# Cross attention's values as seven block products, and recurrence queries with the weights held stationary, in a one-layer decoder kernel

## The chip, the cores and the metric

The kernel runs on one core of a Trainium2 chip. The metric is the device time of one execution in microseconds (us), the median of three timed runs. A profiled execution gives the trace that is read here; its span is the time between the first and the last instruction of the trace.

## The reference

One layer of a hybrid decoder on 256 tokens of width 1024, in float32. What matters here are two of its many products: the queries of the recurrence (`q_b`, 1024 of the 9216 columns of `w_in`) and the values of cross attention to 256 memory tokens (the second half of `wkv`).

```python
xn = rmsnorm(h, norm_mix_g)
q_a, k_a, v_a, q_b, f_b, i_b, og_b, g_a, g_b = split_cols(xn @ w_in)
y_a = moba_attention(q_a, k_a, v_a, positions) @ w_br_attn
y_b = hgrn2(q_b, f_b, i_b, og_b, lb, norm_g) @ w_br_hgrn     # uses silu(q_b) * dk**-0.5
merged = sigmoid(g_a) * y_a + sigmoid(g_b) * y_b
h = x + merged @ w_out
# cross attention, 4 heads of 256
q = rmsnorm(h, norm_x_g) @ wq
kv = rmsnorm(mem, norm_mem_g) @ wkv; k, v = kv[..., :1024], kv[..., 1024:]
p = softmax(q k^T * 256**-0.5);  h = h + (p v) @ wo
h = h + swiglu(rmsnorm(h, norm_ffn_g));  out = rmsnorm(h, final_norm_g)
```

## The kernel before

Every product with a weight keeps float32 accuracy by splitting both factors into a high and a low part of a shorter format, and adding hi·hi, hi·lo and lo·hi on TensorE (PE). The weights lie in DRAM as chunks of 128 x 2048 floats (1 MB). A chunk is loaded by SyncE's queue (SP) into one of three `raw` buffers, ACT copies it into `hi` (two instructions of 128 x 1024, L210), and VectorE (DVE) subtracts into `lo` (two, L211). There are three pairs of `hi`/`lo`. `nxt()` hands out a chunk and lets the chunk two places further on be prepared, so the load of chunk m waits for the `lo` of chunk m-3 (same `raw`), and the `hi` of chunk m waits for PE to be done with chunk m-3 (same `hi`). The list `HEAD` is the order of the 64 chunks ahead of the feed-forward part.

Two routines use a chunk. In `gemm_t` the tokens are stationary and 512 columns of weights move: 24 matmuls of 512 columns, written `pst` (L272 to L274). In `gemm_f` the weights are stationary: 16 pairs of matmuls, one of 512 columns in which the tokens' hi and lo parts stand side by side (L287) and one of 256 (L288), written `psf`; the result has the features on the partitions, and DVE adds its two halves.

- Recurrence queries: two `gemm_t`, four chunks; ACT's Silu by token; then 16 transposes on PE (L486, the function `turned`) put features on the partitions, and DVE and ACT write `QP` and `QQ`.
- Cross attention runs in this order: four `gemm_f` for the keys (here F0 to F3; evictions `ku` on ACT, `kx` on DVE, `kxh` on ACT, `kxl` on GpSimd, which is POOL), one `gemm_t` for half of the values, four `gemm_f` for the queries (Q0 to Q3, the same evictions with `qxh`, `qxl`), and one `gemm_t` for the other half of the values. The scores `xs` of head c are computed behind Q(c+1), those of head 3 in the middle of the last `gemm_t`. DVE takes the row maximum (two instructions on L1046, each with a read of its accumulator), ACT the exponential (L1050), DVE the reciprocal and the scaling of `xp` (L1054), and PE transposes `xp` into `xT` (L1060), one chunk after `xs`. Then come the products with the values, `xo`, and the output weights.

The feed-forward part uses sums of its weight blocks, which `block_sums()` makes in DRAM during the part ahead of it: ACT's queue copies a chunk (L225, L229), and POOL's queue adds another one to it (an accumulating DMA, L231): 15 copies and 15 accumulations. One such step is issued at some of the calls of `nxt()`.

PE's order is the program's. On ACT and DVE, and on POOL for the later half, a scheduler sets the order when the program is built; on the chip each engine then runs its own list strictly in order, DMA issues included. So an instruction that waits holds up all behind it on its engine.

Of the kernel before, what the change touches and what calls it, by code (L numbers as in the profile page):

```python
# [10 lines left out]
F32 = mybir.dt.float32  # L11
F32R = mybir.dt.float32r
# [120 lines left out]
def build(tc, A, out):  # L133
    nc = tc.nc
    V, SC, G, PE, SY = nc.vector, nc.scalar, nc.gpsimd, nc.tensor, nc.sync
    with ExitStack() as ctx:
# [45 lines left out]
        def prep(tags=None, raw=None):  # L182
# [17 lines left out]
            for c in range(sent if 0 < i < len(PIECES) else 0):  # L200
                a = slice(c * 2048 // sent, (c + 1) * 2048 // sent)
                SY.dma_start(raw[:, a], piece(A["w"][i], a))
            if sent == 1:
                SY.dma_start(raw, A["w"][i])
            for c in range(pieces):
                a = slice(c * n, (c + 1) * n)
                if i == 0:
                    SY.dma_start(raw[:, a], piece(A["w"][i], a))
                    yield
                SC.activation(hi[:, a], raw[:, a], AF.Copy)  # L210
                V.tensor_tensor(lo[:, a], raw[:, a], hi[:, a].bitcast(F32), op=ALU.subtract)  # L211
# [7 lines left out]
        summed = [[dram.tile([128, 2048], F32, name="sum%d_%d" % (g, i), tag="sum%d_%d" % (g, i))  # L219
                   for i in range(3)] for g in range(len(PAIRS))]  # L220

        def block_sums():
            for g, (a, b) in enumerate(PAIRS):
                for i in range(2):
                    tc.keep_in_program_order(SC.dma_start(summed[g][i], A["w"][AT_CHUNK["I", b, 0]]))  # L225
                    yield 1
                for i, u in enumerate((("I", a, 0), ("I", b, 1), ("I", b, 1))):
                    if i == 2:
                        tc.keep_in_program_order(SC.dma_start(summed[g][2], summed[g][0]))  # L229
                        yield 1  # L230
                    tc.keep_in_program_order(G.dma_start(  # L231
                        summed[g][i], A["w"][AT_CHUNK[u]], accum_op=ALU.add, max_dma_last_dim=8192))
                    yield 1
# [47 lines left out]
        def gemm_f(X2, evict):  # L281
            w = by_k(nxt(), 8)
            for m in range(2):
                a = slice(m * 128, (m + 1) * 128)
                ps = mm.tile([128, 2, 256], F32, name="psf", tag="mm")
                for k in range(8):
                    PE.matmul(ps, w[0][:, k, a], X2[:, :, k], start=k == 0, stop=False)  # L287
                    PE.matmul(ps[:, 0], w[1][:, k, a], X2[:, 0, k], start=False, stop=k == 7)  # L288
                evict(m, ps)
# [43 lines left out]

        def square(raw, c):
            a = slice(2 * c, 2 * c + 2)
            SC.activation(raw[:, a], raw[:, a], AF.Square)
            if c % 2 == 1:
                b = slice(2 * c - 2, 2 * c)
                V.tensor_tensor(raw[:, a], raw[:, a], raw[:, b], op=ALU.add)

        def feature_sum(raw):
            V.tensor_tensor(raw[:, 2:4], raw[:, 2:4], raw[:, 6:8], op=ALU.add)
            V.tensor_tensor(raw[:, 2], raw[:, 2], raw[:, 3], op=ALU.add)

        def feature_rstd(raw, name):
            ps = bank("ssq", (128, 2))
            for t in range(2):
                PE.matmul(ps[:, t:t + 1], raw[:, 2, t * 128:(t + 1) * 128], ones, start=True, stop=True)
            return rstd_of(ps, name)


        Xh, Xl = big("B1", "Xh", dt=F32R), big("B2", "Xl", dt=F32R)
        X = (Xh, Xl)
# [670 lines left out]
        ph = big("B1", "ph", (128, 4, 2, 256), F32R)
        pl = big("B2", "pl", (128, 4, 2, 256), F32R)

        def ev_vx(c):
            def ev(t, ps):
                a = slice(c * 512, (c + 1) * 512)
                split(ps, vxh[:, t, a], vxl[:, t, a], mem["r"][:, t:t + 1])  # L1030
            return ev
# [32 lines left out]
        for c in range(4):  # L1064
# [132 lines left out]
        def token_sums():  # L1197
            for i in range(4):
                ts[i] = t2("ts", (128, 4, 128))
            V.tensor_tensor(ts[0], gh[1, 0], gh[1, 1], op=ALU.subtract)  # L1200
            V.tensor_tensor(ts[1], ts[0], gh[0, 0], op=ALU.subtract)
            V.tensor_tensor(ts[2], gh[0, 0], gh[1, 0], op=ALU.subtract)
            V.tensor_tensor(ts[3], ts[1], gh[0, 1], op=ALU.add)

# [255 lines left out]
```

## Time and profile before

| | |
|---|---|
| time, median of 3 runs | 614.55 us (614.25 to 614.68) |
| profiled execution | 614.53 us, of it 612.7 us span and 1.8 us around it |
| TensorE clock granted | 0.997 |
| PE busy | 603.5 us |
| DVE / ACT / POOL busy | 445.3 / 369.3 / 116.9 us |
| moved by DMA | 155.7 MB, mean 254 GB/s |

A line of the timeline has the start in us from the span's beginning, the duration, the engine and line, the operation, what it writes and reads with shapes, the count, and in brackets how long the engine stood idle before it and what ended that. Matmuls overlap, so the price of one is the distance between two starts. A line of the windows has the length of the stretch, then the busy time of PE, PE's weight loads, DVE, ACT and POOL with their counts, the granted clock, the DMA engines' mean busy share, and GB/s. A DMA queue's line has packets, MB and the time of its packets as a share of the 16 DMA engines' time; q1 is SP's queue, q10 ACT's, q0 POOL's.

### The profile page before, as it was taken

How to read it: one execution, taken by the hardware profiler on the slowest of the kernel's cores; microseconds unless marked ns; L12 is line 12 of the kernel's file. 1: busy time of each engine (PE TensorE's matmuls, PEld its weight loads, DVE VectorE, ACT ScalarE, POOL GpSimd, SP SyncE). 2: the span in 40 equal slices, each digit the busy share in tenths (PEclk: the TensorE clock that was granted, in tenths of full speed). 3: DMA queues.
4: the chain of work that ended last, by engine and by line, in shares of the span. 5: the costliest groups of instructions: out<-in, count | busy, mean ns of one | idle time of the engine just before them, and what ended most of it. 6: DMA issues, size and time to landing. Idle time of an engine off the chain costs nothing.

```text
span 612.7 us, 8280 instructions
## 1 busy us (share of the span) xinstructions
PE 603.5 (98%) x3075; PEld 501.3 (82%) x3075; DVE 445.3 (73%) x729; ACT 369.3 (60%) x583; POOL 116.9 (19%) x136
## 2 busy tenths in 40 slices
PE   8999999999999999999999999999999999999995
PEld 7888888888887877778878888888888888888884
DVE  7666667988656867655975755786789888888863
ACT  7776444333377666744646656684478767676742
POOL 3887200221200340000221423200000000000003
PEclk9999999999999999999999999999999999999998
DMA  8977968795676567887789888792899989896601
GB/s 344 376 281 285 267 231 236 226 309 227 222 219 213 199 179 206 266 318 275 205 269 297 326 243 247 240 347 93 351 289 329 329 288 327 292 336 214 196 1 68
DMA packets 21832, 155.74 MB, mean 254 GB/s; under 512 B 2736, under 2 KB 3376, under 8 KB 5296
## 3 DMA queue, kind: packets, MB, share of 16 engines
q1 hardware_dynamic: 17712, 117.68, 50.4%
q0 software_dynamic: 2880, 20.97, 17.8%
q10 hardware_dynamic: 1200, 16.57, 7.0%
q8 instruction: 24, 0.39, 0.3%
q14 instruction: 16, 0.13, 0.1%
HBM read 154.16 MB, written 32.51 MB: 305 GB/s over the span
## 4 chain that ended last, share of the span: by engine, by line
PE 93%; DVE 4%; ACT 1%; issue 1%; DMA 1%; POOL 0%; POOLq 0%; DVEq 0%; ACTq 0%
PE pst L272 13%; PE pst L274 13%; PE pst L273 13%; PE bk L272 6%; PE bk L274 6%; PE bk L273 6%; PE psf L287 5%; PE acc L272 3%; PE acc L274 3%; PE acc L273 3%; PE psf L288 2%; PE lp L652 2%; DVE lo L211 1%; PE psg L545 1%; PE pso L274 1%; PE pso L272 1%
## 5 line engine op out<-in xcount | busy, mean ns | idle before, releaser
L211 DVE TENSOR_TENSOR lo<-raw,hi 128x1024 fp32r<-128x1024 f32 (+1 forms) x128 | 155.1, 1228 | 50.9 <-ACT hi L210 50.5
L210 ACT ACTIVATE hi<-raw 128x1024 fp32r<-128x1024 f32 (+1 forms) x128 | 128.2, 1029 | 96.8 <-PE pst L274 72.8
L272 PE MATMUL pst<-hi,Xh 128*128 128x512 f32 x256 | 103.2, 403 | 0.0
L274 PE MATMUL pst<-hi,Xl 128*128 128x512 f32 x256 | 100.0, 390 | 0.0
L273 PE MATMUL pst<-lo,Xh 128*128 128x512 f32 x256 | 99.7, 390 | 0.0
L1165 DVE TENSOR_TENSOR lo<-raw,hi 128x1024 fp32r<-128x1024 f32 x56 | 66.1, 1220 | 12.8 <-ACT hi L1164 12.8
L1164 ACT ACTIVATE hi<-raw 128x1024 fp32r<-128x1024 f32 x56 | 56.3, 1054 | 20.3 <-issue 9.1
L274 PEld LDWEIGHTS pst<-hi,Xl 128*128 128x128 f32 x256 | 48.0, 188 | 10.4
L272 PEld LDWEIGHTS pst<-hi,Xh 128*128 128x128 f32 x256 | 48.1, 188 | 9.9 <-issue 0.7
L273 PEld LDWEIGHTS pst<-lo,Xh 128*128 128x128 f32 x256 | 48.2, 188 | 9.3
L231 POOL DMA_DIRECT2D sum<-w x15 | 13.0, 863 | 78.7 <-DMA sum<-sum 53.1
L1147 POOL DMA_DIRECT2D raw<-w x5 | 4.5, 892 | 119.2 <-DVE lo L1165 33.7
L272 PE MATMUL acc<-hi,hids 128*128 128x512 f32 x64 | 25.1, 392 | 0.0
L274 PE MATMUL acc<-hi,hids 128*128 128x512 f32 x64 | 24.9, 390 | 0.0
L273 PE MATMUL acc<-lo,hids 128*128 128x512 f32 x64 | 24.9, 389 | 0.0
L272 PE MATMUL bk<-hi,Sh 128*128 128x512 f32 x60 | 23.7, 395 | 0.0
L272 PE MATMUL bk<-hi,h2h 128*128 128x512 f32 x60 | 23.7, 394 | 0.0
L274 PE MATMUL bk<-hi,h2l 128*128 128x512 f32 x60 | 23.4, 390 | 0.0
L274 PE MATMUL bk<-hi,Sh 128*128 128x512 f32 x60 | 23.4, 390 | 0.0
L273 PE MATMUL bk<-lo,h2h 128*128 128x512 f32 x60 | 23.4, 389 | 0.0
L273 PE MATMUL bk<-lo,Sh 128*128 128x512 f32 x60 | 23.3, 389 | 0.0
L287 PE MATMUL psf<-H,hi 128*128 128x512 f32 x64 | 22.8, 400 | 0.0
(387 smaller groups left out, 1418.0 us busy)
## 6 DMA issues: line engine op xcount, KB each, us to landing
raw<-w SPq DMA_DIRECT2D x78, 1024.0 KB, 6.3
sum<-w POOLq DMA_DIRECT2D x15, 1024.0 KB, 10.0
raw<-sum SPq DMA_DIRECT2D x13, 1024.0 KB, 6.7
raws<-w SPq DMA_DIRECT2D x11, 1024.0 KB, 5.9
raw<-w POOLq DMA_DIRECT2D x5, 1024.0 KB, 8.4
raw<-w SPq DMA_DIRECT2D x4, 512.0 KB, 6.0
raws<-sum SPq DMA_DIRECT2D x2, 1024.0 KB, 6.1
raw<-w SPq DMA_DIRECT2D x4, 256.0 KB, 4.4
```

Of the source, the lines that this page charges most:

```text
L210: SC.activation(hi[:, a], raw[:, a], AF.Copy)
L211: V.tensor_tensor(lo[:, a], raw[:, a], hi[:, a].bitcast(F32), op=ALU.subtract)
L231: tc.keep_in_program_order(G.dma_start(summed[g][i], A["w"][AT_CHUNK[u]], accum_op=ALU.add, max_dma_last_dim=8192))
L272: PE.matmul(ps, xh, h, start=first, stop=False, skip_group_check=more)
L273: PE.matmul(ps, xh, l, start=False, stop=False, skip_group_check=more)
L274: PE.matmul(ps, xl, h, start=False, stop=last, skip_group_check=more)
L287: PE.matmul(ps, w[0][:, k, a], X2[:, :, k], start=k == 0, stop=False)
L288: PE.matmul(ps[:, 0], w[1][:, k, a], X2[:, 0, k], start=False, stop=k == 7)
L545: PE.matmul(pss[c][t], z[:, k, t * 128:(t + 1) * 128], ws[c][0][:, k], start=z is Xh and k == 0, stop=False)
L652: PE.matmul(ps[:, j], KS[:, a0 + j], QQ[g][:, a0 + j - 8 * g, 0:n], start=True, stop=True)
L1164: SC.activation(hi[:, a], raw[:, a], AF.Copy)
L1165: V.tensor_tensor(lo[:, a], raw[:, a], hi[:, a].bitcast(F32), op=ALU.subtract)
```

## The change

**Values.** The 256 memory tokens and the 1024 x 1024 weights of the values are each taken as 2 x 2 blocks, and the product is made from seven block products instead of eight. One block product, `value_product(p)` (called V1 to V7 below), is one chunk and 12 matmuls of 512 columns, where a whole `gemm_t` chunk has 24. Four of the seven chunks are sums of weights, made in DRAM like the others by `block_sums()`: four more copies, four more accumulations. The token sums are made on POOL (`block_sums_of`, four instructions of 128 x 512, after eight that multiply the memory tokens by their gain) and split by ACT and DVE into `Msh`, `Msl`. The products are combined by DVE in `cv`. V1 and V6 stand behind F0, V7 and V5 behind F1, V3 behind F2; V2 and V4 stand behind Q3, with the scores of head 3 between them. There are 67 chunks in `HEAD` now, and steps of `block_sums()` come at 7 of 10 calls of `nxt()`, before at 6 of 11.

**Recurrence queries.** Four `gemm_f` in place of two `gemm_t` and 16 transposes. For each of eight heads ACT copies, DVE adds and multiplies by the tokens' factors in rows (`x_rows`, made by two small transposes), ACT takes Silu and writes `QQ`, and DVE writes `QP`.

**Layout.** Hi and lo parts of tokens stand side by side for each k; a `gemm_f` then reads 512 neighbouring columns.

```diff
-    for base in (3, 5, 2, 0, 1, 6):
+    order += [("F", "w_in", 3072 + c * 256) for c in range(4)]
+    for base in (5, 2, 0, 1, 6):
...
+    for at, p in zip((1, 2, 4, 5, 7, 13, 14), (1, 6, 7, 5, 3, 2, 4)):
+        out.insert(i + at, ("V", p))
...
+            todo = [(valued, [VALUES[p] for p in (1, 0, 3, 2)])]
...
-            if i >= 4 and (i - 4) * 6 // 11 != (i - 3) * 6 // 11:
+            if i >= 4 and (i - 4) * 7 // 10 != (i - 3) * 7 // 10:
...
-                    PE.matmul(ps, w[0][:, k, a], X2[:, :, k], start=k == 0, stop=False)
+                    PE.matmul(ps, w[0][:, k, a], X2[:, k], start=k == 0, stop=False)
...
-            def ev(t, ps):
-                th[t] = t2("qth")
-                SC.activation(th[t], ps, AF.Silu, scale=r_x[:, t:t + 1])
-                if t == 1:
-                    turned(th, c, use)
+                SC.activation(u, ps[:, 1], AF.Copy)
+                V.tensor_tensor(t, ps[:, 0], u, op=ALU.add)
+                V.tensor_tensor(t, t, x_rows, op=ALU.mult)
+                SC.activation(t, t, AF.Silu)
...
-        for c in range(2):
-            gemm_t(X, ev_q(c))
+        for c in range(4):
+            gemm_f(X2h, ev_q(c))
...
+                G.tensor_scalar(raw[:, k], raw[:, k], gv[:, V_MEM + k:V_MEM + k + 1], None, op0=ALU.mult)
...
-        gemm_t((Mh, Ml), ev_vx(0))
+        def value_product(p):
+            w = by_k(nxt(), 4)
...
+            for k in range(4):
+                mm3t(ps, x[0][:, k], x[1][:, k], w[0][:, k], w[1][:, k], k == 0, k == 3)
+            c1, c6, c7 = (cv[:, i] for i in range(3))
+            if p == 1:
+                SC.activation(c1, ps, AF.Copy)
+            elif p == 6:
+                V.tensor_tensor(c6, ps, c1, op=ALU.add)
+            elif p == 7:
+                V.tensor_tensor(c7, ps, c6, op=ALU.add)
+            elif p == 5:
+                d = t2("vd")
+                V.tensor_tensor(d, ps, c7, op=ALU.subtract)
+                V.tensor_tensor(c6, ps, c6, op=ALU.subtract)
+                value_out(0, 1, d)
...
+        for c, ps_ in enumerate(((1, 6), (7, 5), (3,), ())):
+            gemm_f(M2, ev_sum(kxh, kxl, c))
+            for p in ps_:
+                value_product(p)
...
-        gemm_t((Mh, Ml), ev_vx(1))
+        for p in (2, 4):
+            value_product(p)
```

The schedulers' lists change with it. POOL around the keys and queries, before: `kxl` and `qxl` are evictions of keys and queries, `sum` the accumulations for the feed-forward part.

```order
L323 TENSOR_TENSOR r_h_3075<-v__3073,nhalf 128x2
L1017 TENSOR_TENSOR kxl<-kx,kxh 128x256 x8
L231 DMA sum_0_111<-w 128x2048
L1017 TENSOR_TENSOR qxl<-kx,qxh 128x256 x2
L231 DMA sum_1_112<-w 128x2048
L1017 TENSOR_TENSOR qxl<-kx,qxh 128x256 x6
L231 DMA sum_2_113<-w 128x2048
```

The same place now:

```order
L354 TENSOR_TENSOR r_h_3185<-v__3183,nhalf 128x2
L1050 TENSOR_TENSOR kxl<-kx,kxh 128x256 x4
L262 DMA sum_0_111<-w 128x2048
L262 DMA sum_2_110<-w 128x2048
L1050 TENSOR_TENSOR kxl<-kx,kxh 128x256 x2
L262 DMA sum_1_112<-w 128x2048
L1050 TENSOR_TENSOR kxl<-kx,kxh 128x256 x2
L1050 TENSOR_TENSOR qxl<-kx,qxh 128x256 x2
L262 DMA sum_2_113<-w 128x2048
```

Before, one accumulation stands behind the keys' evictions and the next one chunk later; now two stand behind the evictions of F1, and a third behind those of F2.

ACT from the end of the keys on, before (`ku`, `kxh`, `qxh` evictions; `hi` the split of coming chunks):

```order
L1016 ACTIVATE kxh<-kx 128x256 x2
L210 ACTIVATE hi<-raw 128x1024 x3
L316 ACTIVATE vxh<-pst,r_m 128x512 x2
L210 ACTIVATE hi<-raw 128x1024 x2
L1013 ACTIVATE ku<-psf 128x256
L1016 ACTIVATE qxh<-kx 128x256
L210 ACTIVATE hi<-raw 128x1024
```

The same place now; the first two `hi` are those of Q1, the next two (one row each) those of Q2, the last two those of Q3:

```order
L229 ACTIVATE hi<-raw 128x1024 x2
L347 ACTIVATE vxh<-cv,r_m 128x512
L262 DMA sum_2_113<-sum_0_111 16x16384
L1046 ACTIVATE ku<-psf 128x256 x2
L229 ACTIVATE hi<-raw 128x1024
L1049 ACTIVATE kxh<-kx 128x256 x2
L229 ACTIVATE hi<-raw 128x1024
L1046 ACTIVATE ku<-psf 128x256
L229 ACTIVATE hi<-raw 128x1024
L1049 ACTIVATE qxh<-kx 128x256
L1046 ACTIVATE ku<-psf 128x256
L229 ACTIVATE hi<-raw 128x1024
```

Before, the copy that reads `sum_0_111` stood behind the evictions of Q0 and Q1, out of the piece shown; now it stands ahead of those of F3. The evictions of Q0 (the last two `ku` and the `qxh`) stand behind both halves of Q2's split and among those of Q3's.

DVE at the end of cross attention, before, from the row maximum of head 3 to its scaled `xp`:

```order
L1046 ISA xmx 128x1
L211 TENSOR_TENSOR lo<-raw,hi 128x1024
L1048 SCALAR_TENSOR_TENSOR xmx<-xmx,r_3070 128x2
L314 TENSOR_TENSOR pl<-xT,ph 128x512
L211 TENSOR_TENSOR lox<-raw,hix 128x1024
L1052 RECIPROCAL xsum<-xsum 128x2
L211 TENSOR_TENSOR lox<-raw,hix 128x1024
L1054 TENSOR_SCALAR xp<-xp,xsum 128x256 x2
```

And now:

```order
L1114 ISA xmx 128x1
L348 SCALAR_TENSOR_TENSOR vxl<-cv,r_m,vxh 128x512
L1116 SCALAR_TENSOR_TENSOR xmx<-xmx,r_3180 128x2
L230 TENSOR_TENSOR lo<-raw,hi 128x1024
L345 TENSOR_TENSOR ph<-xT,ph 128x512
L1120 RECIPROCAL xsum<-xsum 128x2
L230 TENSOR_TENSOR lo<-raw,hi 128x1024
L1122 TENSOR_SCALAR xp<-xp,xsum 128x256 x2
```

The same kinds of work stand between the maximum and `xp`; on PE, 12 matmuls of V4 stand beside it where there were 24 of `gemm_t`.

More of the change, by code (lines that the diff above doesn't have):

```diff
@@ L69, with head @@
 AT_CHUNK = {u: i for i, u in enumerate(ORDER)}
-HEAD = [i for i, u in enumerate(ORDER) if u[0] not in "IO"]
+VALUES = {p: ("T", "wkv_x", 1024 + c * 512, kh) for p, (c, kh) in
+          {1: (1, 0), 2: (1, 1), 3: (0, 1), 0: (0, 0)}.items()}
+def head():
+    out = [u for u in ORDER if u[0] not in "IO" and u not in VALUES.values()]
+    i = out.index(("F", "wkv_x", 0))
+    for at, p in zip((1, 2, 4, 5, 7, 13, 14), (1, 6, 7, 5, 3, 2, 4)):
+        out.insert(i + at, ("V", p))
+    return out
+HEAD = head()
 PAIRS = [(o, o + 1) for o in range(1, NF // 2, 2)]
@@ L207, in prep @@
                 if i == 0:
-                    SY.dma_start(raw[:, a], piece(A["w"][i], a))
+                    SY.dma_start(raw[:, a], piece(src, a))
                     yield
@@ L218, in build, with four_of @@
         dram = pool("dram", 1, space=bass.MemoryType.DRAM)
-        summed = [[dram.tile([128, 2048], F32, name="sum%d_%d" % (g, i), tag="sum%d_%d" % (g, i))
-                   for i in range(3)] for g in range(len(PAIRS))]
+        def four_of(name, n):
+            return [dram.tile([128, 2048], F32, name=name + str(i), tag=name + str(i)) for i in range(n)]
+        summed = [four_of("sum%d_" % g, 3) for g in range(len(PAIRS))]
+        valued = four_of("val", 4)
         def block_sums():
-            for g, (a, b) in enumerate(PAIRS):
-                for i in range(2):
-                    tc.keep_in_program_order(SC.dma_start(summed[g][i], A["w"][AT_CHUNK["I", b, 0]]))
-                    yield 1
[L227 to L233, printed above, removed]
+            todo = [(valued, [VALUES[p] for p in (1, 0, 3, 2)])]
+            todo += [(summed[g], [("I", a, 0), ("I", b, 0), ("I", b, 1)]) for g, (a, b) in enumerate(PAIRS)]
+            steps = []
+            for g, (to, units) in enumerate(todo):
+                w = [A["w"][AT_CHUNK[u]] for u in units]
+                for i in range(len(to)):
+                    src = (w[1], w[1], to[0], to[2])[i]
+                    steps.append(((g, i, 0), (g, (0, 0, 0, 2)[i], 1) if i > 1 else None, SC, to[i], src, {}))
+                    steps.append(((g, i, 1), (g, i, 0), G, to[i], (w[0], w[2], w[2], w[-1])[i],
+                                  dict(accum_op=ALU.add, max_dma_last_dim=8192)))
+            done = {None: -9}
+            for n in range(len(steps) * 2):
+                free = [z for z in steps if done.get(z[1], n) <= n - 3]
+                if free:
+                    z = free[0]
+                    steps.remove(z)
+                    done[z[0]] = n
+                    tc.keep_in_program_order(z[2].dma_start(z[3], z[4], **z[5]))
+                    yield 1
+            assert not steps
         sums = block_sums()
@@ L332, in rows_of @@
             return o
[L334 to L352, printed above, removed]
+        X2h = big("B1", "Xh", (128, 8, 2, 256), F32R)
+        Xh, Xl = X2h[:, :, 0], X2h[:, :, 1]
         X = (Xh, Xl)
@@ L572, in build @@
             ev(t, pss[1][t])
+        x_rows = rows_of(r_x, "x", "rowsB")
         tick()
@@ L932, in memory @@
             yield 1
+            sq = []
             for k in range(8):
-                split(raw[:, k], Mh[:, k], Ml[:, k], gv[:, V_MEM + k:V_MEM + k + 1])
-                if k % 2 == 1:
-                    square(raw, k // 2)
+                if k % 2 == 0:
+                    j = (t2b if k else t2)("msq", (128, 2, 256))
+                    SC.activation(j, raw[:, k:k + 2], AF.Square)
+                    sq.append(j)
+                    if k:
+                        V.tensor_tensor(sq[0], sq[0], j, op=ALU.add)
+                G.tensor_scalar(raw[:, k], raw[:, k], gv[:, V_MEM + k:V_MEM + k + 1], None, op0=ALU.mult)
+                split(raw[:, k], Mh[:, k], Ml[:, k])
                 if k in (2, 5, 7):
                     yield 1
-            feature_sum(raw)
+            V.tensor_tensor(sq[0][:, 0], sq[0][:, 0], sq[0][:, 1], op=ALU.add)
+            g = {(t, c): raw[:, 4 * c:4 * c + 4, t * 128:(t + 1) * 128] for t in range(2) for c in range(2)}
+            ts = block_sums_of(g, G)
             yield 1
-            mem["r"] = feature_rstd(raw, "m")
+            ps = bank("ssq", (128, 2))
+            for t in range(2):
+                PE.matmul(ps[:, t:t + 1], sq[0][:, 0, t * 128:(t + 1) * 128], ones, start=True, stop=True)
+            mem["r"] = rstd_of(ps, "m")
+            for i in range(4):
+                split(ts[i], Msh[:, i], Msl[:, i])
             yield 1
@@ L1006, in build @@
         kxl = big("B11", "kxl", dt=F32R)
-        qxh = big("B12", "qxh", dt=F32R)
-        qxl = big("B6", "qxl", dt=F32R)
         def ev_sum(dh, dl, c):
@@ L1018, in ev_sum @@
             return ev
-        for c in range(4):
-            gemm_f(M2, ev_sum(kxh, kxl, c))
         vxh = big("B7", "vxh", (128, 2, 1024), F32R)
         vxl = big("B14", "vxl", (128, 2, 1024), F32R)
[L1024 to L1031, printed above, removed]
@@ L1033, in build, with value_out @@
-        gemm_t((Mh, Ml), ev_vx(0))
+        cv = big("B4", "cv", (128, 3, 512))
+        probs = big("B1", "ph", (128, 4, 2, 2, 256), F32R)
+        ph, pl = probs[:, :, 0], probs[:, :, 1]
+        def value_out(c, t, src):
+            a = slice(c * 512, (c + 1) * 512)
+            split(src, vxh[:, t, a], vxl[:, t, a], mem["r"][:, t:t + 1])
+        def value_product(p):
+            w = by_k(nxt(), 4)
+            ps = mm.tile([128, 512], F32, name="psv", tag="mm")
+            if p in (1, 2, 4):
+                kh, t = {1: (0, 0), 2: (1, 0), 4: (1, 1)}[p]
+                x = [z[:, 4 * kh:4 * kh + 4, t * 128:(t + 1) * 128] for z in (Mh, Ml)]
+            else:
+                x = [z[:, {5: 0, 6: 1, 7: 2, 3: 3}[p]] for z in (Msh, Msl)]
+            for k in range(4):
[12 more added lines that the diff above has]
+                value_out(0, 1, d)
+            elif p == 3:
+                V.tensor_tensor(c6, ps, c6, op=ALU.add)
+                value_out(0, 0, c6)
+            elif p == 2:
+                V.tensor_tensor(c1, ps, c1, op=ALU.add)
+                value_out(1, 0, c1)
+            else:
+                V.tensor_tensor(c7, ps, c7, op=ALU.add)
+                value_out(1, 1, c7)
+            tick()
@@ L1034, in build @@
+        for c, ps_ in enumerate(((1, 6), (7, 5), (3,), ())):
+            gemm_f(M2, ev_sum(kxh, kxl, c))
+            for p in ps_:
+                value_product(p)
         drain(h1g)
+        qxh = big("B12", "qxh", dt=F32R)
+        qxl = big("B6", "qxl", dt=F32R)
         def scores(x):
@@ L1197, in token_sums @@
         def token_sums():
[L1198 to L1203, printed above, removed]
+            ts.update(enumerate(block_sums_of(gh, V)))
         def sum_parts(*which):
```

52 lines of the change are left out of this document (34 added, 18 removed).

## The prediction

> **What bounds the kernel.** I read the page's shares first, then the chain that ended last, then PE's waits.
>
> ```profile
> span 612.7 us, 8280 instructions
> PE 603.5 (98%) x3075; PEld 501.3 (82%) x3075; DVE 445.3 (73%) x729; ACT 369.3 (60%) x583; POOL 116.9 (19%) x136
> PE 93%; DVE 4%; ACT 1%; issue 1%; DMA 1%; POOL 0%; POOLq 0%; DVEq 0%; ACTq 0%
> ...
> PE as L803 <- ACT pT L829: 0.5, 1, 0.5
> PE mT L901 <- POOL tat L896: 0.2, 1, 0.2
> ...
> PE xT L1060 <- DVE xp L1054: 0.2, 1, 0.2
> ```
>
> PE is busy 603.5 of 612.7 us and makes 93% of the chain. In mid-kernel it waits for 0.5, 0.2 and 0.2 us, no more. So a matmul less is time gained, as long as everything that feeds PE keeps up. The sum is made against the profiled execution, 614.53 us, which is the median of the runs but for 0.02.
>
> **Recurrence queries.**
>
> ```profile
> 27.54 0.60 PE L486 MATMUL fT__411<-cst,fth 128*128 128x128 f32 x4
> ...
> 28.33 0.48 PE L272 MATMUL pst<-hi,Xh 128*128 128x512 f32 x1
> 28.64 0.40 PE L273 MATMUL pst<-lo,Xh 128*128 128x512 f32 x1
> 28.88 0.39 PE L274 MATMUL pst<-hi,Xl 128*128 128x512 f32 x1
> ...
> 33.64 0.39 PE L274 MATMUL pst<-hi,Xl 128*128 128x512 f32 x1
> 329.33 0.38 PE L329 MATMUL rb<-cst,r_m 128*128 128x128 f32 x2
> 329.47 0.48 PE L287 MATMUL psf<-M,hi 128*128 128x512 f32 x1
> 336.33 0.40 PE L287 MATMUL psf<-M,hi 128*128 128x512 f32 x1
> ...
> 352.28 0.40 PE L287 MATMUL psf<-M,hi 128*128 128x512 f32 x1
> ```
>
> From 28.88 to 33.64 are 21 matmuls of 512 columns, 0.2267 us each, so a `gemm_t` chunk of 24 is 5.44 us. From 336.33 to 352.28 are 46 pairs, 0.3467 each, so a `gemm_f` chunk of 16 is 5.55. Eight transposes take 27.54 to 28.33, and the matmul behind them 0.31 instead of 0.23: 0.87 together. Removed: 4 x 5.44 + 2 x 0.87 = 23.5. Added: 4 x 5.55 = 22.2, and the two transposes for `x_rows`, 0.14 as in 329.33 to 329.47 and some 0.1 for the matmul behind. Together -1.1 us.
> ```profile
> 28.00:60.00 32.00, 32.00 (x162) 26.96 (x161) 20.41 (x24) 22.78 (x31) 26.55 (x39) 1.00 0.71 272
> ```
>
> DVE gets 24 instructions of 128 x 256 where four of twice the width stood (some +7 us at 0.4 and 0.7 each), ACT 24 where eight stood (+5). In this stage, 28 to 60, both have about 10 of 32 us free and the chunk in use was prepared two earlier: 0. If that cover is gone, PE waits for one `lo`, about 1 us. The new layout moves the same columns: 0.
>
> **Values, on PE.** 84 matmuls instead of 96: 12 x 0.2267 = -2.7 us. The waits of 0.5 and 0.2 stand where the orders of ACT and POOL change; they were small accidents, and I take -0.5 (0 to -0.7).
>
> **Values, what feeds PE.** Three more chunks to load and split, four more copies, four more accumulations. From F0's start the old stretch had six chunks in 33 us; the new one has nine up to F3's end, in about 36.7 us (4 x 5.55 + 5 x 2.72 + 0.9 for eight transposes of h1), one each 4.1 us.
>
> ```profile
> q1 hardware_dynamic: 17712, 117.68, 50.4%
> q0 software_dynamic: 2880, 20.97, 17.8%
> q10 hardware_dynamic: 1200, 16.57, 7.0%
> ...
> 330.00:363.00 33.00, 33.00 (x181) 28.52 (x180) 21.00 (x29) 19.75 (x36) 12.55 (x10) 1.00 0.84 284
> ...
> raw<-w SPq DMA_DIRECT2D x1, 1024.0 KB, 5.3
> ...
> sum<-w POOLq DMA_DIRECT2D x1, 1024.0 KB, 10.4
> raw<-w SPq DMA_DIRECT2D x1, 1024.0 KB, 10.4
> ...
> q0 software_dynamic: 58, 0.48, 77.9%
> q1 hardware_dynamic: 48, 0.39, 32.3%
> ```
>
> The shares of the queues over 612.7 us give the engine time of 1.05 MB: a load 2.75 us, an accumulation 5.45, a copy 2.8. The window of the old stretch shows the DMA engines 84% busy already, DVE 21 of 33 us. DVE gets 6 `lo` (1.2 each) and five combinations (0.7): 32 of 36.7, still below. The DMA engines don't stay below: 3 loads more are 8 us, and more of the sums' steps fall into it. A load alone landed 5.3 us after its issue (issued in 333 to 338), beside an accumulation 10.4 (323 to 328). The last two rows are 398 to 401 us, when both were in flight: in 3 us the accumulation moved 0.48 MB and the load 0.39, so a load takes 8.1 us there, an accumulation 6.6.
>
> The Trainium skill, "DMA: Bandwidth & Descriptors", section "Queues, rings and completion order", says that each DMA engine takes its queues in turn, a packet from each. The trace nearly agrees (58 packets against 48); with even turns a load would take 7.2 us, and the sum below would be about 1 us lower.
>
> Now the order. POOL issues the accumulations of `sum_0_111` and `sum_2_110` right after the four `kxl` of F0 and F1. DVE reaches F1's `kx` only behind `cv<-psv` of V7. With 0 at F0's start, PE ends F0 with h1's transposes at 6.4, F1 at 17.4, V7 at 20.2, V5 at 22.9, F2 at 28.4, V3 at 31.1, F3 at 36.7, Q0 at 42.2, Q1 at 47.8.
>
> ```profile
> 334.65 0.42 DVE L1014 TENSOR_TENSOR kx<-psf,ku 128x256 f32<-128x256 f32 x1
> 335.60 0.73 POOL L1017 TENSOR_TENSOR kxl<-kx,kxh 128x256 fp32r<-128x256 f32 x1 [2.20 <-ACT kxh L1016]
> 342.96 0.71 ACT L1016 ACTIVATE kxh<-kx 128x256 fp32r<-128x256 f32 x2
> 405.15 2.01 ACT L210 ACTIVATE hix<-raw 128x1024 fp32r<-128x1024 f32 x2 [1.95 <-DMA raw<-w]
> ```
>
> V7's end, `cv` 0.7, `kx` 2 x 0.4, `kxh` 0.7 and `kxl` 2 x 0.7: POOL issues both at about 24. The first lands near 34.4 (10.4), its last 6.6 us moving, and the second 6.6 later at 41. The third, behind F2's `kxl`, is issued near 38 and lands at 47.6. So from about 28 to 47.6 loads go at 8.1 us each. Load Q0 is issued when F2's `lo` is done (24.7, since DVE has `vd` of V5 between its halves) and starts behind F3's load near 26: two thirds of it fast, the rest slow, landing near 31. Q1 follows near 39, Q2 at 47, Q3 at full speed near 50, or 53 if ACT's copy of `sum_0_111` (2.8) falls beside it. ACT has both halves of Q2's split and Q3's first ahead of Q0's `qxh`, and Q3's second ahead of the other `qxh`. So the scores of head 0 need landing Q3 + 2 x 1.0 + `ku`, 2 `kxh`, `kxl` (1.7) = 54 to 57, and PE has nothing left from Q1's end, 47.8, on. That is 6 to 9 us; I take 7.5. The row 405.15 is the same wait in small: ACT stood 1.95 us before `hix` for a load beside an accumulation. F2 adds 0.4 (its second `lo` behind `vd`). Bounds: 0 if loads land as fast as alone (Q3 at 41, ready at 45), 12 if copies and accumulations fall together.
>
> **End of cross attention.**
>
> ```profile
> 398.23 0.60 PE L1060 MATMUL xT<-cst,xp 128*128 128x128 f32 x4
> 398.58 0.48 PE L272 MATMUL pst<-hi,M 128*128 128x512 f32 x1
> ...
> 404.50 0.81 PE L1060 MATMUL xT<-cst,xp 128*128 128x128 f32 x4 [0.21 <-DVE xp L1054]
> 399.27 0.42 DVE L1046 CUSTOM_DVE_ANT_0 xp<-xs,rows_m 128x256 f32<-128x256 f32 x1
> ...
> 399.96 1.22 DVE L211 TENSOR_TENSOR lo<-raw,hi 128x1024 fp32r<-128x1024 f32 x1
> 401.10 0.15 DVE L1048 SCALAR_TENSOR_TENSOR xmx<-xmx,r 128x2 f32<-128x2 f32 x1
> 401.17 0.69 DVE L314 TENSOR_TENSOR pl<-xT,ph 128x512 fp32r<-128x512 f32 x1
> ...
> 404.10 0.61 DVE L1054 TENSOR_SCALAR xp<-xp,xsum 128x256 f32<-128x256 f32 x2
> 404.62 0.75 DVE L317 SCALAR_TENSOR_TENSOR vxl<-pst,r_m,vxh 128x512 fp32r<-128x512 f32 x1
> 401.35 0.60 ACT L1050 ACTIVATE xp<-xp,xmx,r 128x256 f32<-128x256 f32 x1
> ```
>
> Head 3's softmax runs from the scores' end, 398.23, to 404.50, 6.3 us, in which DVE also does three or four `lo`, `pl` and more; 24 matmuls (5.44) covered all but 0.21. Now 12 cover it (2.72), and V2's `cv` with head 2's scaling stands ahead of the maximum. DVE from the scores' end: maximum 0.75, `vxl` 0.7, `xmx` 0.1, `lo` 1.15, `pl` 0.65, reciprocal 0.1, `lo` 1.15, `xp` half 0.3: about 4.9 against 0.35 + 2.72 of PE. That is 1.8, and 0.3 at head 2: 2.1 where 0.2 was, +1.9 (1 to 3.3, the whole 2.7 uncovered and some).
>
> **Sum.** -1.1 - 2.7 - 0.5 + 7.5 + 0.4 + 1.9 = +5.5: 614.5 + 5.5 = 620.0 us. With the scores' stall at 5 to 12 and the ends of the others, 617 to 624.5.
>
> **Rivals.**
> - *The loads keep ahead*: 0 for the stall and F2's 0.4 + 1.9 kept: 612.5 us. It decides where load Q3 lands by about 44 on the scale above. For it: loads landed in 5.3 us alone, and the three `raw` buffers let a load go two chunks ahead. Against: accumulations of 1 MB hold the engines for 20 us in a row, which the old order avoided.
> - *All hidden*: also no stall at the end of cross attention: 614.5 - 4.3 = 610.2. The row with 0.21 speaks against: no slack is left there.
> - *Half*: the accumulations come earlier or apart, the stall is 2 to 4: 614 to 617.
> - *The memory tokens' stage*:
>
> ```profile
> 265.00:280.00 15.00, 15.00 (x71) 11.92 (x70) 8.20 (x10) 5.71 (x8) 0.00 (x0) 1.00 0.76 279
> ```
>
>   POOL gets 12 instructions there ahead of `tat`, for which PE waited 0.2 before. Should they and an accumulation's issue delay `tat`, each us there is one of PE, on top: over 624.5 with the stall. In the old trace (265 to 280) POOL did nothing and DVE was busy 8.2 of 15 us, so I hold it for small.
> - *Not what it says*: that the seven products don't save 12 matmuls is excluded by the code.
>
> **Chances.** Scores held by loads 0.55 (617 to 624.5); half 0.15; loads ahead 0.17; all hidden 0.08; beyond 624.5 0.05. A change under 0.2%, 1.2 us, can't be told from none. Faster takes the third and fourth, 0.25; same takes two thirds of "half" and some of the next, 0.13; slower the rest, 0.62. The range from 612.3 to 624.5 leaves out the fourth and the last, 0.13 together, and a bit of the third.
>
> **What would show it.** In the new profile: PE busy about 4 us less; among PE's waits `xs` behind POOL's `kxl`/`qxl` with several us, ACT idle ahead of `hi` for DMA, loads of 8 us and more between F2 and Q3, and `xT` behind `xp` with 1 to 2 us. If `xs` does not wait and loads there land in 5 to 7 us, the middle term is wrong and 612.5 is near.

## The result: 1.1% slower, by loads that arrive late

| | before | after |
|---|---|---|
| time, median (range) | 614.62 us (614.25 to 614.82) | 621.31 us (620.10 to 622.62) |
| profiled execution, span | 614.53, 612.7 us | 622.62, 620.8 us |

The ratio is 1.0108, with an interval of 1.0094 to 1.0122: 6.7 us slower where 5.5 were forecast. The page of the kernel after begins:

```profile
span 620.8 us, 8403 instructions
PE 602.3 (97%) x3081; PEld 499.4 (80%) x3081; DVE 464.4 (75%) x766; ACT 380.0 (61%) x611; POOL 136.6 (22%) x152
q1 hardware_dynamic: 18144, 120.82, 50.3%
q0 software_dynamic: 3456, 25.17, 20.5%
q10 hardware_dynamic: 1328, 20.76, 8.6%
PE 85%; DMA 7%; DVE 4%; issue 1%; ACT 1%; POOL 0%; POOLq 0%; ACTq 0%; DVEq 0%
...
raw<-w SPq DMA_DIRECT2D x77, 1024.0 KB, 7.3
sum<-w POOLq DMA_DIRECT2D x15, 1024.0 KB, 14.5
```

PE works 1.2 us less, yet the span is 8.1 us longer. DMA has gone from 1% to 7% of the chain that ended last; a load lands in the median 7.3 us after its issue instead of 6.3, an accumulation 14.5 instead of 10.0. PE's waits, then ACT's for loads after, then ACT's for loads before (`hix` is the `hi` of the output weights):

```profile
PE xT L1128 <- DVE xp L1122: 3.2, 4, 1.4
PE xs L305 <- POOL qxl L1050: 1.9, 2, 1.0
...
PE psf L318 <- DVE kx L1047: 1.5, 1, 1.5
PE psf L319 <- DVE lo L230: 1.4, 2, 0.8
PE pst L303 <- ACT mh L344: 1.1, 1, 1.1
PE pst L305 <- DVE mh L345: 0.6, 1, 0.6
```
```profile
ACT hi L229 <- DMA raw<-w: 23.6, 9, 7.0
```
```profile
ACT hix L210 <- DMA raw<-w: 2.0, 1, 2.0
...
ACT hi L210 <- DMA raw<-w: 1.5, 2, 1.3
```

The names on the right are the last links only. Behind `qxl`, `kx` and `lo` stands ACT, which over the whole execution waited 23.6 us for loads ahead of `hi`, and in whose list those `hi` stand ahead of the evictions. Such a wait costs PE nothing by itself: in run 1 below ACT has 10.1 us of them, and PE no wait above 0.2 us in mid-kernel.

Where the time went shows in the stretch from F0's start to the first `xo`, by the starts of these two on PE: 329.47 to 405.07 before, 329.85 to 413.06 after. One line each, before first; the columns are length, PE, weight loads, DVE, ACT, POOL, granted clock, DMA share, GB/s.

```profile
329.47:405.07 75.60, 75.39 (x428) 65.38 (x426) 51.11 (x88) 46.91 (x87) 21.19 (x20) 1.00 0.85 269
```
```profile
329.85:413.06 83.21, 75.19 (x416) 63.45 (x413) 58.79 (x99) 53.15 (x95) 20.49 (x21) 1.00 0.86 289
```

12 matmuls fewer, and 7.6 us longer: nearly all of the net loss lies here. Up to F0 the kernel after is 0.4 us late (it had been 1.5 us ahead at the merge's first transposes, `mT`, 298.5 against 297.0, and lost that to the two `pst` waits); behind `xo` the two run alike, 199.6 before against 199.4 us after, to the start of the last group of `bk`.

POOL's lines in the stretch, then DMA issues there (the last column is the median time to landing; five windows, which begin at 354.1, 355, 357, 361 and 370.5), then ACT's `hi`:

```profile
351.98 2.23 POOL L1050 TENSOR_TENSOR kxl<-kx,kxh 128x256 fp32r<-128x256 f32 x2 [13.49 <-ACT kxh L1049]
354.16 1.72 POOL L262 DMA_DIRECT2D sum<-w  x2
...
371.76 0.78 POOL L262 DMA_DIRECT2D sum<-w  x1
```
```profile
sum<-w POOLq DMA_DIRECT2D x1, 1024.0 KB, 9.1
...
raw<-w SPq DMA_DIRECT2D x1, 1024.0 KB, 11.7
...
raw<-w SPq DMA_DIRECT2D x1, 1024.0 KB, 14.3
...
raw<-w SPq DMA_DIRECT2D x1, 1024.0 KB, 13.2
...
raw<-w SPq DMA_DIRECT2D x1, 1024.0 KB, 9.9
```
```profile
367.06 2.01 ACT L229 ACTIVATE hi<-raw 128x1024 fp32r<-128x1024 f32 x2 [7.01 <-DMA raw<-w]
371.98 1.06 ACT L229 ACTIVATE hi<-raw 128x1024 fp32r<-128x1024 f32 x1 [2.30 <-DMA raw<-w]
...
380.58 1.06 ACT L229 ACTIVATE hi<-raw 128x1024 fp32r<-128x1024 f32 x1 [2.14 <-DMA raw<-w]
```

Two accumulations are issued back to back, pinned behind F1's `kxl`; they land after 9.1 and 15.9 us. The loads of Q0, Q1, Q2 and Q3, issued at 355.32, 357.59, 361.12 and 370.54, land after 11.7, 14.3, 13.2 and 9.9 us, and ACT stands before each.

### The profile page after: what moved, and what is told of

Its sections match the earlier page's. It is cut to its first block, busy times and chain, and to the rows that moved or that the text cites. A ratio compares the mean times of both kernels' runs of the same rounds, so it can differ in the third digit from the quotient of the medians.

```text
span 620.8 us, 8403 instructions
## 1 busy us (share of the span) xinstructions
PE 602.3 (97%) x3081; PEld 499.4 (80%) x3081; DVE 464.4 (75%) x766; ACT 380.0 (61%) x611; POOL 136.6 (22%) x152
## 4 chain that ended last, share of the span: by engine, by line
PE 85%; DMA 7%; DVE 4%; issue 1%; ACT 1%; POOL 0%; POOLq 0%; ACTq 0%; DVEq 0%
PE pst L303 11%; PE pst L305 11%; PE pst L304 11%; DMA raw<-w 7%; PE bk L303 6%; PE bk L305 6%; PE bk L304 6%; PE psf L318 4%; PE acc L303 3%; PE acc L304 3%; PE acc L305 3%; PE psf L319 2%; DVE lo L230 2%; PE lp L665 2%; PE psg L557 1%; PE pso L303 1%
## 5 line engine op out<-in xcount | busy, mean ns | idle before, releaser
L230 DVE TENSOR_TENSOR lo<-raw,hi 128x1024 fp32r<-128x1024 f32 (+1 forms) x134 | 162.6, 1231 | 47.8 <-ACT hi L229 47.6
L229 ACT ACTIVATE hi<-raw 128x1024 fp32r<-128x1024 f32 (+1 forms) x134 | 134.1, 1030 | 100.4 <-PE pst L305 69.3
L303 PE MATMUL pst<-hi,Xh 128*128 128x512 f32 x224 | 90.5, 404 | 0.0
L305 PE MATMUL pst<-hi,Xh 128*128 128x512 f32 x224 | 87.5, 391 | 0.0
L304 PE MATMUL pst<-lo,Xh 128*128 128x512 f32 x224 | 87.2, 389 | 0.0
L305 PEld LDWEIGHTS pst<-hi,Xh 128*128 128x128 f32 x224 | 42.0, 188 | 9.1
L303 PEld LDWEIGHTS pst<-hi,Xh 128*128 128x128 f32 x224 | 42.1, 188 | 8.8 <-issue 0.7
L304 PEld LDWEIGHTS pst<-lo,Xh 128*128 128x128 f32 x224 | 42.1, 188 | 8.1
L303 PE MATMUL bk<-hi,h2h 128*128 128x512 f32 x60 | 23.6, 394 | 0.0
L305 PE MATMUL bk<-hi,h2h 128*128 128x512 f32 x60 | 23.4, 390 | 0.0
L318 PE MATMUL psf<-M,hi 128*128 128x512 f32 x64 | 22.8, 398 | 0.0
## 6 DMA issues: line engine op xcount, KB each, us to landing
sum<-w POOLq DMA_DIRECT2D x15, 1024.0 KB, 14.5
val<-w POOLq DMA_DIRECT2D x4, 1024.0 KB, 10.1
```

The source lines that it names most:

```text
L303: PE.matmul(ps, xh, h, start=first, stop=False, skip_group_check=more)
L304: PE.matmul(ps, xh, l, start=False, stop=False, skip_group_check=more)
L305: PE.matmul(ps, xl, h, start=False, stop=last, skip_group_check=more)
L318: PE.matmul(ps, w[0][:, k, a], X2[:, k], start=k == 0, stop=False)
```

## The experiments

**1. Values undone.** `gemm_t` for the values again, 64 chunks, 30 steps at 6 of 11 calls, no token sums. Kept: queries, layout, memory tokens' gain on POOL.

```diff
-            todo = [(valued, [VALUES[p] for p in (1, 0, 3, 2)])]
-            todo += [(summed[g], [("I", a, 0), ("I", b, 0), ("I", b, 1)]) for g, (a, b) in enumerate(PAIRS)]
+            todo = [(summed[g], [("I", a, 0), ("I", b, 0), ("I", b, 1)]) for g, (a, b) in enumerate(PAIRS)]
...
-            if i >= 4 and (i - 4) * 7 // 10 != (i - 3) * 7 // 10:
+            if i >= 4 and (i - 4) * 6 // 11 != (i - 3) * 6 // 11:
...
-            for p in ps_:
-                value_product(p)
+        gemm_t((Mh, Ml), ev_vx(0))
...
-        for p in (2, 4):
-            value_product(p)
+        gemm_t((Mh, Ml), ev_vx(1))
```

> The changed kernel with its values put back to two gemm_t chunks pairs (64 chunks, 30 steps of block sums at 6 of 11 calls, no token sums); the queries, the layout and the gain on POOL stay as changed. Theory A (the loss is the values': accumulations back to back starve the weight loads): 0.8 below the kernel before, 613.8 us (613.2 to 614.4), and no wait of PE above 0.6 us in cross attention. Theory B (the new layout or the queries carry a part of the loss): above 615.

Measured: 612.41 us, ratio 0.9959 (0.9943 to 0.9974), below what was expected. In the stretch:

```profile
327.20:402.80 75.60, 75.39 (x427) 65.38 (x426) 51.09 (x88) 47.29 (x88) 21.16 (x20) 1.00 0.81 264
```

The old 75.60 again. So the values cost 621.31 - 612.41 = 8.9 us (9.2 by the two ratios to the kernel before), and what is left is faster than both kernels, the fastest tried that computes all of the reference.

**2. Fewer sums.** The kernel after, but the sums of the last two pairs of the feed-forward part aren't made.

```diff
-            todo += [(summed[g], [("I", a, 0), ("I", b, 0), ("I", b, 1)]) for g, (a, b) in enumerate(PAIRS)]
+            todo += [(summed[g], [("I", a, 0), ("I", b, 0), ("I", b, 1)]) for g, (a, b) in enumerate(PAIRS[:3])]
...
```

> The changed kernel without the sums of the last two pairs of the feed-forward part: 12 of 38 steps (6 copies, 6 accumulations) are left out, and the feed-forward part loads plain weights in their place, so its output lacks those sums; every chunk, split, matmul and combination stays. Theory A: without accumulations between F1 and Q3 loads land in 5 to 8 us, the 8.7 us of waits there and the 1.8 at the merge's transposes go, the 2.2 at the end of cross attention stay: 611 us (609.8 to 613). Theory B (DVE and ACT can't keep up with three more chunks and the combinations): 619 to 621.

Measured: 611.64 us, ratio 0.9944 (0.9924 to 0.9963). The stretch, its DMA issues, and PE's waits:

```profile
327.65:402.58 74.93, 73.31 (x415) 63.29 (x413) 57.81 (x99) 54.10 (x95) 16.43 (x17) 1.00 0.58 208
```
```profile
raw<-w SPq DMA_DIRECT2D x8, 1024.0 KB, 4.8
raw<-val SPq DMA_DIRECT2D x2, 1024.0 KB, 4.7
```
```profile
PE xT L1128 <- DVE xp L1122: 1.6, 2, 1.4
...
```

None of the sums' DMAs falls into the stretch now; the loads land in 4.8 us, and of the waits in the kernel after only those of `xT` are left; the merge's are gone too. It gives the two terms apart: 83.21 - 74.93 = 8.3 us is the stall by late loads, and 74.93 against 75.60 is all that the seven products bring when nothing is late, 0.7 us. Copies and accumulations are taken away together here; no run tells their shares of the stall apart.

**3. The control.** The same 12 steps left out of the kernel before (same edit).

> Control: the kernel before with the sums of the last two pairs left out (12 of 30 steps), plain weights loaded in their place, so its output lacks those sums. Theory A: before, the accumulations were hidden, so nothing or little is gained: 614.0 us (613.4 to 614.7). If it gains as much as the changed kernel did without them (9.7), the sums cost the same in both and the values' part is not what made them dear.

Measured: 614.35 us, ratio 0.9992 (0.9982 to 1.0001); the stretch takes 75.60, loads in it 4.8 us. So the DMAs of these 12 steps were hidden before: without the three more chunks they cost nothing that the times show.

**4. Seven products without the value sums.** V4 to V7 load plain weights; eight steps of `block_sums()` fewer, 6 of 11 calls.

```diff
-                src = valued[{5: 0, 7: 1, 6: 2, 4: 3}[u[1]]]
+                src = A["w"][AT_CHUNK[VALUES[{5: 0, 7: 1, 6: 2, 4: 3}[u[1]]]]]
...
```

> The changed kernel without the four sums of the values' weights: V4 to V7 load plain weights (the values are wrong sums), 30 steps at 6 of 11 calls as before the change; all seven products, their chunks and the rest stay. POOL's list has one accumulation behind F1's evictions, one behind F2's, one behind Q0's. Theory A (what matters is accumulations close together while a chunk is due every 4 us): part of the stall stays, 2 to 5 us, 615 us (613 to 617). Rival (the eight added steps alone are the cause): as good as without the last two pairs' sums, 611.2 to 612.2.

Measured: 619.04 us, ratio 1.0069 (1.0054 to 1.0084), above what was expected.

```profile
326.94:409.35 82.41, 77.27 (x416) 65.73 (x414) 59.70 (x99) 53.29 (x95) 20.77 (x20) 0.96 0.80 274
```
```profile
PE xT L1127 <- DVE xp L1121: 3.9, 4, 2.0
...
PE psf L318 <- DVE lo L230: 0.6, 1, 0.6
PE xs L302 <- ACT qxh L1048: 0.4, 1, 0.4
```

F0 starts at 326.94, and the merge has no wait: its 2.2 us belong to the eight more steps. The stretch is nearly as long as with them. But the clock stood at 0.50 for 6.8 us in it (section on the hardware below), and PE is busy 2.1 us more than in the kernel after. So of 82.41 - 74.93 = 7.5 us some 2 to 3 may be clock; another execution of this kernel with nearly full clock took the same 619.07, so this isn't split cleanly. When the clock fell, 4.2 us had been lost against run 2: the first `xT` starts 61.14 us behind F0, there 56.97. So three more chunks beside as many accumulations as before are enough for a stall of 4 to 7.5 us:

| in the stretch | 12 chunks | 15 chunks |
|---|---|---|
| no DMA of the sums | 75.60 (run 3) | 74.93 (run 2) |
| three accumulations, three copies | 75.60 (before and run 1) | 82.41 (run 4) |
| four and four | | 83.21 (after) |

In this stretch it takes both. It does not take two accumulations in a row: in run 4 they are issued one by one, at 351.27, 367.14 and 380.00, before at 357.70, 373.92 and 393.54.

**5. Queries undone too** (on top of run 1): layout, order of steps, squares and gain on POOL are left.

```diff
-        for c in range(4):
-            gemm_f(X2h, ev_q(c))
+        for c in range(2):
+            gemm_t(X, ev_q(c))
```

> The kernel with values undone, and the recurrence queries put back too (two gemm_t and 16 transposes): what is left of the change is the layout, the new order of the block sums' steps, the squares in their own tile and the gain on POOL. If the queries are worth 0.8 as the trace of before to after shows: 613.2 us (612.6 to 613.8). If they carry all of the 2.4 gained with values undone: 614.8.

Measured: 613.71 us, ratio 0.9986 (0.9976 to 0.9995). Queries: 613.71 - 612.41 = 1.3 by the medians, 1.7 by the two ratios, 0.6 by F0's start in the two traces (327.77 against 327.20); their gain is no better known than that. Layout and orders: 614.54 - 613.71 = 0.8; the wait for `as` is gone.

**6. V3 later**, between V2 and V4, to give the loads of Q0 to Q3 one chunk less ahead.

```diff
-    for at, p in zip((1, 2, 4, 5, 7, 13, 14), (1, 6, 7, 5, 3, 2, 4)):
+    for at, p in zip((1, 2, 4, 5, 12, 13, 14), (1, 6, 7, 5, 2, 3, 4)):
...
-        for c, ps_ in enumerate(((1, 6), (7, 5), (3,), ())):
+        for c, ps_ in enumerate(((1, 6), (7, 5), (), ())):
...
-        for p in (2, 4):
+        for p in (2, 3, 4):
```

> The changed kernel with V3 moved from behind F2 to between V2 and V4, its token sum kept in spare room; all else the same. Theory A: 24 matmuls cover head 3's softmax again, so the 1.6 us wait of xT there goes to 0.2; one chunk less in the crowded stretch lets each load of Q0 to Q3 come one place earlier, 2 to 4 us less stall: 617.5 us (615.5 to 619.5). Theory B (the stall is the engines' work, and the end wait is set by DVE's list): 620.5 to 621.5.

Measured: 627.02 us, ratio 1.0203 (1.0178 to 1.0229). A miss of 9.5 us. The stretch fell to 79.7, as expected of it, but F0 started at 338.9.

```profile
PE pst L303 <- ACT mh L344: 4.3, 3, 1.9
```
```profile
304.64 1.06 ACT L229 ACTIVATE hi<-raw 128x1024 fp32r<-128x1024 f32 x1 [10.05 <-DMA raw<-w]
```

The token sum of V3 needed another place in the memory, and its split moved up in ACT's list, ahead of a `hi`: it starts at 278.62, after ACT has waited 10.17 us there for POOL's `ts`; in the kernel after it starts at 308.15. All behind it is late, loads land after 15.9 to 20.6 us, and ACT stands another 10.05 us for one of them. Nor did head 3's softmax get 24 matmuls as cover: its `xT` stands behind V3, ahead of V4, and `xT` still waits 2.0 us. The run tells nothing of V3's place; it tells what one instruction too early in a list can cost.

**7. Steps spread** so that few DMAs of the sums fall between F0 and Q0: 33 up to the 44th call, then none, five from Q0 on.

```diff
+        def quota(i):
+            return (min(i, 44) - 4) * 5 // 6 + max(0, min(i, 62) - 57)
...
-            if i >= 4 and (i - 4) * 7 // 10 != (i - 3) * 7 // 10:
+            if i >= 4 and quota(i) != quota(i + 1):
```

> The changed kernel with the 38 steps of the block sums issued at other calls: 33 up to call 43, none from there to F3's end, the last five one by one from Q0 on; same DMAs, same matmuls. Theory A: the stall between F2 and Q3 falls from 8.7 to 1 to 3 us and the merge's 1.8 may stay or go, 614 us (612.5 to 616.5). Theory B: 620 to 622, the time does not depend on when the steps are issued.

Measured: 617.89 us, ratio 1.0048 (1.0031 to 1.0066), above what was expected.

```profile
PE xT L1131 <- DVE xp L1125: 4.2, 2, 3.1
...
```

No wait from F0 to Q3, where loads land in 4.7 to 5.7 us: half of the loss is gone. The other half has moved: four accumulations from 370 to 396 make the loads at the end of cross attention late (11.9 to 15.5 us), and PE waits for the softmax of heads 2 and 3. In head 3's, three splits of coming chunks, 3.6 us, stand between the maximum and `xp` in DVE's list, one more than in the kernel after.

**8. `xT` of head 3 later**, behind `xo` of the first two heads.

```diff
+            if x == 3:
+                yield 1
             pT = bank("xT", (128, 2, 256))
```

> The changed kernel with one edit: PE's transposes xT of head 3 come behind the products xo of heads 0 and 1 (24 matmuls of 256 columns, 2.9 us) instead of behind V4. Theory A (PE waits there because 12 matmuls don't cover the softmax): the 1.6 us wait goes, all else stays: 1.4 below the changed kernel, 619.9 us (619 to 620.8). Theory B (the wait is set by DVE, which also does the values' last split and is late with them all the same): no change, 621.3, and the wait shows up at xo or xT again.

Measured: 622.45 us (619.73 to 626.71), ratio 1.0134 (1.0090 to 1.0177): no answer by the time, since the runs differ by 7 us. The profile answers for the place alone. From the scores of head 3 to the first `xo` it is 5.2 us instead of 7.3, but head 3's `xT` stands behind that now; to the first product with the output weights (`pso`) it is 12.6 instead of 13.1. So the edit gains 0.5 us there, not the 1.4 of theory A. The rest has moved to `xo`, as theory B has it; the waits left are

```profile
PE xT L1130 <- DVE xp L1122: 0.5, 2, 0.3
PE xo L300 <- DVE vxl L348: 0.5, 1, 0.5
```

**9. Copies and accumulations in turn**, so that no two accumulations stand together in the order of steps.

```diff
...
-                    z = free[0]
+                    z = ([z for z in free if z[2] is not last[0]] or free)[0]
+                    last[0] = z[2]
```

> The changed kernel with the same 38 steps of block sums at the same calls of nxt, but in another order: copies and accumulations alternate, where they came three and three. Theory A (accumulations in a row starve the loads): fewer waits at the merge (1.8 goes to 0 to 0.5); in the stretch three accumulations still stand close on POOL, so half the stall stays: 617.5 us (615 to 620). Theory B (only their total counts): 621.

Measured: 626.08 us, ratio 1.0188 (1.0171 to 1.0205), a miss of 8.6. In turn in the program isn't in turn on the chip: the stretch got five accumulations, where the kernel after has four: one issued at 333.26 ahead of F0's `kxl`, then two together at 351.73, one at 369.55 and one at 388.32.

```profile
PE xs L304 <- ACT qxh L1050: 4.5, 1, 4.5
PE psf L319 <- DVE kx L1048: 3.3, 2, 2.7
```

**10. All three** (7 with 35 steps up to the 44th call and three from Q0 on, 8, 9).

> The changed kernel, whole computation, with three edits: steps alternate, 35 of the 38 are issued by call 44 and the last three from Q0 on, and xT of head 3 stands behind xo of head 1. Theory A: no accumulation is issued between F0 and F3 but one behind F3's evictions, one behind Q3's; stall 0 to 2 us, merge 0 to 1, end 0: 611.5 us (610 to 613.5), below both kernels. Theory B: 619 or more.

Measured: 620.04 us, ratio 1.0084 (1.0069 to 1.0099), a miss of 8.5.

```profile
PE xo L302 <- ACT vxh L351: 2.3, 1, 2.3
PE lp L669 <- DVE ATS L676: 2.1, 3, 1.5
PE ao L853 <- ACT pT L846: 1.9, 1, 1.9
```

Up to the first `xo` the stretch takes 73.4, but here head 3's `xT` stands behind that. Up to the first `pso` it takes 84.1, against 89.0 in the kernel after, 80.8 in run 2 and 81.5 before: `xo` waits, and the clock stood at 0.50 for 3.4 us. And `mT` starts at 302.5 instead of 297.0: the steps brought forward take 5.5 us further ahead, in the recurrence (`lp`) and in attention (`ao`). In none of the placements tried did every stage have room for the eight steps.

## Why the prediction was right, point by point

| term | predicted | measured |
|---|---|---|
| queries | -1.1 | -1.3 by the medians (run 5 against 1), -0.8 over that stage in the trace |
| 12 matmuls | -2.7 | -2.7 by count |
| small waits | -0.5 | -0.8 (run 5, with layout and orders) |
| stall of the scores and F2 | +7.9 | +8.3 (after against run 2), of it 6.4 up to the end of head 0's scores |
| end of cross attention | +1.9 | +2.0, what is left of run 2 against run 1, 74.93 - 75.60 + 2.72; the waits of `xT` alone +1.4 (1.6 against 0.2) |
| memory tokens, merge | held for small | +2.2: F0 at 329.85 against 327.65 in run 2 |
| sum | +5.5 | +7.7 by these; medians +6.7, profiled execution +8.1 |

*What feeds PE* was right in its mechanism, loads made late by the sums' DMAs and three more chunks, and ACT's list that passes it on; runs 1 to 4 show it. POOL's issue of two accumulations was put at 24 us behind F0, 353.9 on this clock; it came at 354.16. Of the landings predicted, Q1 (369) and Q2 (377) came within 3 us, at 371.9 and 374.3, and Q3 (380 to 383) at 380.4. Q0 was wrong: put at 361 on the ground that two thirds of it would move fast, it landed at 367.0. Therefore the stall isn't the one wait ahead of head 0's scores of which the text speaks. By the starts of PE's groups, against run 2, 0.9 us are lost in F2, 3.1 from there to the end of Q1, 2.5 in head 0's scores, and 1.9 ahead of head 0's `xT`, a place that has no price in the prediction. Up to the end of head 0's scores that is 6.4 us, not 7.9; that the whole came so near is partly luck. The stall was worked out from two accumulations in a row, and those aren't needed (run 4); nor are they enough, since in the kernel after a pair issued at 163.91 and 164.47 cost PE no wait. And the load read as alone, with 5.3 us, had an accumulation beside it until 336.47; run 2 has 4.8.

Of the signs named, ACT's waits for loads, loads of 8 us and more, and `xT` with 1.4 us came. `xs` waited 1.9 us, not several. PE is busy 1.2 us less, not 4: its busy time grows with the waits, 75.19 us in the stretch against 73.31 in run 2, which has the same matmuls there.

*End of cross attention* was right in place and nearly in size, and run 2 shows that it is no contention: its 1.4 us wait for `xp` stays when every load is fast. The cause is read from the trace: head 3's softmax takes 5.3 us from the end of its scores at 407.2 to `xT` at 412.49, and PE has 3.2 us of work in that time; DVE works without a pause, 2.4 us of it on two `lo`. No edit shows it: run 8, which took the wait away at `xT`, got only 0.5 us back, so DVE's list has its part. The wait in the kernel after:

```profile
412.49 0.81 PE L1128 MATMUL xT<-cst,xp 128*128 128x128 f32 x4 [1.37 <-DVE xp L1122]
```

*The memory tokens' stage* is the term that failed. It stood among the rivals with the price left open and "I hold it for small", on the ground that POOL was idle there and DVE had room. It was asked there whether POOL's work delays `tat`; it does not, no such wait is in the profile. What came is the same starvation of loads as in cross attention, one stage earlier, ahead of `mh`. ACT, then PE:

```profile
312.14 1.06 ACT L229 ACTIVATE hi<-raw 128x1024 fp32r<-128x1024 f32 x1 [3.37 <-DMA raw<-w]
313.10 0.58 ACT L344 ACTIVATE mh<-mT 128x512 fp32r<-128x512 f32 x1
```
```profile
313.73 0.50 PE L303 MATMUL pst<-hi,mh 128*128 128x512 f32 x1 [1.15 <-ACT mh L344]
...
315.11 0.50 PE L305 MATMUL pst<-hi,mh 128*128 128x512 f32 x1 [0.64 <-DVE mh L345]
```

Loads and steps of the sums were counted for the stretch around the values only; eight more steps come at all calls of `nxt()` from the fifth on, and the count should have been made for each stage. With 2.2 for it the same sum would have come to 622.2; the forecast was near the median of 621.31 without it, and four executions of the kernel after lie between 620.10 and 622.62.

*Queries* came out as worked, in the trace 0.3 less than it: a `gemm_f` chunk in that stage took 17.03 / 3 = 5.68 us, not the 5.55 taken from the keys' stage.

The rivals: loads ahead (612.5) and all hidden (610.2) are what run 2 does when 12 steps are taken away, 611.64. They were no wrong pictures of PE, but they need loads that land in 4.8 us; the DMA engines are 58% busy in that stretch, 86% in the kernel after.

## What to carry to other kernels

Saving matmuls by loading more is worth the matmuls only where the DMA engines have the time: add up their engine time for each stage, background transfers included, before counting matmuls, and try the change once without the background (run 2), which prices both at once. The mean share of a stretch that stalls hides the lack, as the stall lengthens it: 0.86 of 83.21 us is 71.6 us of the engines' time, 96% of the 74.93 us that PE needs when nothing is late. In run 4 it is 0.80 of 82.41, 88%, and before it was 85%, without a stall. Background transfers that are pinned behind other instructions on in-order engines can come in bunches, and moving them moves the stall: each of the three placements of the steps tried here (runs 7, 9 and 10) lost time elsewhere. Where a product that covers another chain (a softmax) is halved, price the uncovered chain as its own term.

## What the runs showed of the hardware

- A load of 1 MB lands in 4.8 us with no copy or accumulation beside it (run 2). In the kernel after, the loads of Q0 to Q3 took 9.9 to 14.3 beside accumulations, in run 6 one took 20.6 with several queued; the four accumulations of the stretch took 9.1 to 15.9. The mean DMA share was only 0.86 there: a stage can starve with the mean below full.

- A stall can be followed by half the clock. In run 9 PE waited 4.5 us from 382.6 on. The same columns as above, ahead of the wait, from its last us on, and later:

```profile
380.00:382.60 2.60, 2.60 (x17) 2.17 (x15) 0.00 (x0) 0.26 (x1) 0.80 (x2) 1.00 1.02 277
386.00:392.00 6.00, 4.36 (x15) 3.78 (x16) 4.57 (x11) 3.97 (x8) 2.86 (x4) 0.50 0.74 276
393.00:399.00 6.00, 6.00 (x42) 5.44 (x41) 3.48 (x7) 3.99 (x9) 0.80 (x1) 1.00 0.99 276
```

  The granted clock fell to 0.50 for 6.8 us. It did so too in the profiled executions of runs 4, 6, 7, 8 and 10, for 3.4 or 6.8 us each time. In run 8 a stretch of 3.6 us with 1.30 of PE's work was enough, and no wait in it was longer than 1.66:

```profile
314.60:318.20 3.60, 1.30 (x5) 0.50 (x4) 2.08 (x3) 2.49 (x3) 0.00 (x0) 1.00 1.00 332
318.40:321.60 3.20, 3.20 (x9) 2.55 (x8) 1.27 (x2) 0.72 (x2) 0.00 (x0) 0.50 0.99 381
```

  In the profiled execution of the kernel after, where no wait in mid-kernel is longer than 1.5, no stall was followed by it. The Trainium skill, "TensorE: Matmul & The Clock Gate", section "What's actually happening", tells of a gate that halves the clock after an idle window of about 3.4 us, and lets it go after a busy one. The lengths of 3.4 and 6.8 us agree; that PE has to be idle for a window doesn't, by the row with 1.30 of 3.60 us. How much of the misses of runs 4, 6, 7, 9 and 10 it accounts for isn't settled, as runs of one kernel with and without the drop took nearly the same time (run 4: 619.03 at a mean clock of 0.991, 619.07 at 0.996).
